# Queries and keys split into high and low part behind the transposition instead of ahead of it

## Chip, cores, metric

One core of a Trainium2 chip. The metric is the device time of one execution in microseconds, the median of the runs of a kernel; lower is better. Five engines work side by side, each on its own queue in order: TensorE (PE, its weight loads shown as PEld), VectorE (DVE), ScalarE (ACT), GpSimd (POOL), SyncE (SP, which issues nearly all DMAs here).

## The reference

Two pre-norm residual layers on x (256 tokens, 2048 channels, fp32). Layer A is sliding-window attention (window 128), layer B is native sparse attention: a compressed, a selected and a windowed branch, mixed by sigmoid gates. Both have 32 query heads of 64 dims in 4 key/value groups, a rotary embedding on the first 16 dims of queries and keys, and a SiLU gate ahead of the output projection:

```
proj = h @ w_in                                   # h = rmsnorm(x)
q = apply_rope(q, cos, sin);  k = apply_rope(k, cos, sin)
s = einsum('bqghd,bkgd->bghqk', q, k) * hd**-0.5  # then mask, softmax (A: with sinks)
o = einsum('bghqk,bkgd->bqghd', p, v)
x = x + (o * silu(z)) @ w_out
```

With 256 tokens all four blocks of 64 keys are selected, so the selected branch of B is plain causal attention.

## The kernel before

**Number format.** The projections and the scores run on PE in fp32r (a reduced fp32 that PE takes at full rate). To keep fp32 accuracy a tensor is split into a high part (an ACT copy that rounds to fp32r) and a low part (a DVE subtraction of the high part), and the products hi*hi, lo*hi, hi*lo are summed in PSUM. Weights are split this way too: `w_hi` by ACT and `w_lo` by DVE for each 512 KB block that arrives (`split`, L549).

**Loops.** The program is a list of steps, each a block of weights: for layer A keys and values, then for each of 4 groups the 512 query columns and the 512 gate columns (z), then the output projection; layer B likewise, with a small MLP that compresses keys and values and a gate projection in between. The products of a step with the activations make the `acc` matmuls. Attention runs in the background of these steps in units (g, t), g a group of 8 heads, t a tile of 128 tokens, so 8 units in each layer. A unit's front (`a_front` L812, `b_front` L1195) transposes its queries, multiplies them with the keys (tiles `s`) and does the softmax; its back transposes the probabilities (`pT`, fp32, with the fp32 identity, which lies in the tile `cst`), multiplies with the values (`pv`) and, in `finalize` (L706), applies the gate and splits the result into `aT_hi` and `aT_lo` for the output projection. In layer B the compressed branch adds the transposition `pcT` and the product `pv<-pcT,vbd`.

**Queries.** `post_q` (L627) runs when the projection of a group's queries for one token tile stands in PSUM: ACT copies it out with its scale (`q32`), POOL applies the rotation (`rope`, L613), ACT writes the high part and DVE the low part, both into one tile `qs` that holds high and low of each head side by side (128 columns a head). `q_transposed` (L639) then transposes each head's 128 columns, so that the high part lies on partitions 0 to 63 and the low part on 64 to 127 of `qT`: 8 fp32r transpositions with `identr` into two PSUM banks, and one ACT copy of each bank. A product with the keys, whose tile holds the same key part on both halves of the partitions, then sums high and low of the query at once.

**Keys.** `post_kv` (L666) does the same for 4 key heads: `key_stack` (L650) writes high (ACT) and low (DVE), each twice side by side, and `keys_to` (L658) transposes 4 + 4 blocks in fp32r into two banks with one ACT copy each. It runs for two token tiles in layer A, and for two in each of two key sets in layer B: 6 times.

**Buffers.** The ring `qs` has 2 tiles (4 KB a partition), the ring `q32` 2 (2 KB; also used by `side`, `th`, `low`, `junk`), the ring `qT` 2, the projection's PSUM banks `acc` 3, and the PSUM banks for all transpositions (`t_bank`, L357) 2.

**Order.** All instructions are recorded first. `Plan.order` (L247) then sets the order on each engine by simulating the queues with prices from `_price` (L164; a DVE instruction with 512 elements is priced at 612 ns there, a transposition in fp32 at about twice one in fp32r). Of the instructions of an engine that are ready by its clock, the one recorded first is taken; the weight splits go ahead of all, and `acc` matmuls fill what is left. PE work is treated as ready 0.8 us later than its inputs. So another price or another dependency moves rows far from the lines that were edited. The names of tiles in the trace are those of the program; since every instruction is recorded through one helper, all have the line L217.

Of the kernel before, what the change touches and what calls it, by code (L numbers as in the profile page):

```python
# [12 lines left out]
F32 = mybir.dt.float32  # L13
F32R = mybir.dt.float32r
# [6 lines left out]
P = 128  # L21
# [4 lines left out]
NG = 4  # L26
HPG = 8
HD = 64
NB = 512
# [310 lines left out]
def trunk(ctx: ExitStack, tc: tile.TileContext, x, positions, norm_w, final_norm_w,  # L340
# [4 lines left out]
    PE, ACT, DVE, POOL, SP = (Engine(plan, n, e) for n, e in (  # L345
        ("PE", nc.tensor), ("ACT", nc.scalar), ("DVE", nc.vector), ("POOL", nc.gpsimd), ("SP", nc.sync)))
    sb = Ring(plan, ctx.enter_context(tc.tile_pool(name="sb", bufs=1)))
# [6 lines left out]
    def s_bank(name):  # L354
        return pp.tile([P, NB], F32, tag="s", name=name, bufs=2)

    def t_bank(name, dt=F32):  # L357
        return pp.tile([P, 4, P], dt, tag="t", name=name, bufs=2)
# [4 lines left out]
    def copy(out, in_, scale=1.0):  # L363
        ACT.activation(out, in_, AF.Copy, scale=scale)
# [7 lines left out]
    ps = s_bank("idle")  # L372
# [8 lines left out]
    ident = cst[:, 0:P]  # L381
# [12 lines left out]
    identr = sb.tile([P, P], F32R, name="identr")  # L394
# [12 lines left out]
    for i, shift in enumerate((0.0, 0.25)):  # L407
# [3 lines left out]
        src = ang  # L411
        for c in TWO_PI:
            DVE.scalar_tensor_tensor(red[:, i], rnd[:, i], -c, src, op0=OP.mult, op1=OP.add)
            src = red[:, i]
# [37 lines left out]
    tb = t_bank("nwT")  # L452
# [4 lines left out]
    urgent, queue = deque(), deque()  # L457
# [40 lines left out]
    rq = [sb.tile([P, NT], F32, name=f"rq{i}") for i in range(2)]  # L498
# [114 lines left out]
    def rope(v, t, nh):  # L613

        tmp = sb.tile([P, 2, HPG, 16], F32, tag="rope", name="rope")
        a, b = tmp[:, 0, 0:nh, :], tmp[:, 1, 0:nh, :]

        def bc(tab, lo, n):
            return tab[:, t].rearrange("p a b -> p (a b)")[:, None, lo:lo + n].to_broadcast([P, nh, n])
        POOL.tensor_tensor(out=a, in0=v[:, :, 0:16], in1=bc(cs, 0, 16), op=OP.mult)  # L620
        POOL.tensor_tensor(out=b[:, :, 0:8], in0=v[:, :, 8:16], in1=bc(sn, 0, 8), op=OP.mult)
        POOL.tensor_tensor(out=b[:, :, 8:16], in0=v[:, :, 0:8], in1=bc(sn, 8, 8), op=OP.mult)
        POOL.tensor_tensor(out=v[:, :, 0:16], in0=a, in1=b, op=OP.add)

    qs = {}

    def post_q(layer, g):  # L627
        def post(t, ps):
            q32 = sb.tile([P, HPG, HD], F32, tag="q32", name="q32", bufs=2)
            copy(q32.rearrange("p h d -> p (h d)"), ps, scale=rq[layer][:, t:t + 1])  # L630
            rope(q32, t, HPG)
            s = sb.tile([P, HPG, 2, HD], F32R, tag="qs", name="qs", bufs=2)
            copy(s[:, :, 0, :], q32)
            DVE.tensor_sub(s[:, :, 1, :], q32, s[:, :, 0, :])
            qs[layer, g, t] = s
            flags.add(("q", layer, g, t))
        return post

    def q_transposed(layer, g, t):  # L639
        s = qs.pop((layer, g, t))  # L640
        qT = sb.tile([P, HPG, P], F32R, tag="qT", name="qT", bufs=2)
        for h in range(2):
            tb = t_bank("qT", F32R)
            for i in range(4):
                PE.transpose(tb[:, i, :], s[:, 4 * h + i].rearrange("p a d -> p (a d)"), identr)
            copy(qT[:, 4 * h:4 * h + 4, :], tb.bitcast(F32))
            yield 230.0
        return qT

    def key_stack(k32, n, name):  # L650

        s = sb.tile([P, 2, NG, 2, HD], F32R, tag="qs", name=name, bufs=2)
        src = k32[0:n, :, None, :].to_broadcast([n, NG, 2, HD])
        copy(s[0:n, 0], src)
        DVE.tensor_sub(s[0:n, 1], src, s[0:n, 0])
        return s

    def keys_to(kT, s, off):  # L658
        for hl in range(2):
            tb = t_bank("kT", F32R)  # L660
            for g in range(NG):
                PE.transpose(tb[:, g, :], s[:, hl, g].rearrange("p a d -> p (a d)"), identr)
            copy(kT[:, :, hl, off:off + P], tb.bitcast(F32))
            yield 230.0

    def post_kv(layer, kT, offs, vt):  # L666
        def post(t, ps):
            k32 = sb.tile([P, HPG, HD], F32, tag="q32", name="k32", bufs=2)[:, 0:NG]
            copy(k32.rearrange("p h d -> p (h d)"), ps[:, 0:256], scale=rms[layer][:, t:t + 1])
            DVE.tensor_scalar(vt()[:, t, :], ps[:, 256:512], rms[layer][:, t:t + 1], None, op0=OP.mult)  # L670
            rope(k32, t, NG)
            s = key_stack(k32, P, "kstack")
            urgent.append(keys_to(kT(), s, offs[t]))
        return post


# [135 lines left out]
    def a_front(g, t, kT, box):  # L812
        while ("q", 0, g, t) not in flags:
            yield None
        qT = yield from q_transposed(0, g, t)
        sms = []
        for par in range(2):
            sm = [sm_tile()]
            nm = sb.tile([P, 4], F32, tag="nm", name="nm", bufs=4)
            den = sb.tile([P, 4], F32, tag="den", name="den", bufs=4)  # L820
            yield from a_scores(g, t, kT, qT, par, sm, nm, den)
            sms.append(sm)
        box.append(sms)
# [371 lines left out]
    def b_front(g, t, box):  # L1195
        while ("q", 1, g, t) not in flags or "kcmp" not in flags or "gate" not in flags:
            yield None
        qT = yield from q_transposed(1, g, t)
        sms = []
        sc = sb.tile([P, HPG, 16], F32, tag="sc", name="sc", bufs=2)  # L1200
        for par in range(2):
            sm = [sm_tile() for _ in range(2)]
            nm = sb.tile([P, 2, 4], F32, tag="nmb", name="nmb", bufs=4)
            den = sb.tile([P, 2, 4], F32, tag="denb", name="denb", bufs=4)
            yield from b_scores(g, t, qT, par, sm, nm, den, sc)
            sms.append(sm)
        pc = cmp_softmax(g, t, sc)
        yield 0.0
        box.append((sms, pc))
# [73 lines left out]
    n = len(steps)  # L1283
# [72 lines left out]
```

## Time and profile before

| | |
|---|---|
| median of 3 runs | 799.94 us (799.88 to 800.97) |
| the profiled execution | 801.18 us, its span 799.5 us |
| PE busy | 783.0 us (98%), 4092 matmuls |
| DVE busy | 553.8 us (69%) |
| ACT busy | 479.1 us (60%) |
| POOL busy | 125.5 us (16%) |
| granted PE clock | 0.998 on average |
| DMA | 128.77 MB, mean 161 GB/s |

The page has the busy time of each engine, the chain of work that ended last (followed back from the last instruction through whatever released each step), and groups of instructions by operation and tile. PE's matmuls overlap in the records: a row's own duration is longer than the distance to the next row's start. What PE work costs is therefore read from the starts of rows that follow each other, or from the chain, whose pieces add up to the span.

### The profile page before, as it was taken

How to read it: one execution, taken by the hardware profiler on the slowest of the kernel's cores; microseconds unless marked ns; L12 is line 12 of the kernel's file. 1: busy time of each engine (PE TensorE's matmuls, PEld its weight loads, DVE VectorE, ACT ScalarE, POOL GpSimd, SP SyncE). 2: the span in 40 equal slices, each digit the busy share in tenths (PEclk: the TensorE clock that was granted, in tenths of full speed). 3: DMA queues.
4: the chain of work that ended last, by engine and by line, in shares of the span. 5: the costliest groups of instructions: out<-in, count | busy, mean ns of one | idle time of the engine just before them, and what ended most of it. 6: DMA issues, size and time to landing. Idle time of an engine off the chain costs nothing.

```text
span 799.5 us, 11784 instructions
## 1 busy us (share of the span) xinstructions
PE 783.0 (98%) x4092; PEld 631.8 (79%) x4092; DVE 553.8 (69%) x1148; ACT 479.1 (60%) x963; POOL 125.5 (16%) x169
## 2 busy tenths in 40 slices
PE   7999999999999999999999999999999999999995
PEld 4888878788788788888878887778868768777884
DVE  5657958858779655556756478858959868885572
ACT  6658657557476445554756486667658748654452
POOL 2102311213023000020101021111211021120110
PEclk9999999999999999999999999999999999999999
DMA  8655454654653555566667653544444444364652
GB/s 271 186 181 162 131 185 129 183 159 117 180 178 132 177 185 185 182 192 172 197 204 218 184 159 106 159 109 130 132 131 134 109 127 133 109 208 131 189 181 105
DMA packets 85995, 128.77 MB, mean 161 GB/s; under 512 B 6178, under 2 KB 43265, under 8 KB 85808
## 3 DMA queue, kind: packets, MB, share of 16 engines
q1 hardware_dynamic: 85536, 126.72, 52.4%
q0 software_dynamic: 400, 1.30, 0.6%
q8 instruction: 32, 0.52, 0.3%
q14 instruction: 27, 0.22, 0.1%
HBM read 125.91 MB, written 2.10 MB: 160 GB/s over the span
## 4 chain that ended last, share of the span: by engine, by line
PE 92%; DVE 3%; issue 2%; ACT 1%; DMA 1%; POOL 1%; SPq 0%; ACTq 0%; POOLq 0%; DVEq 0%
PE acc L217 75%; PE pv L217 5%; PE s L217 4%; PE pT L217 4%; PE qT L217 1%; DVE w_lo L217 1%; PE xT L217 1%; DMA raw<-in_a_w_in 1%; DVE sm L217 1%; ACT w_hi L217 1%; PE gates L217 1%; PE pcT L217 0%; PE kT L217 0%; PE mlp L217 0%; POOL rope L217 0%
## 5 line engine op out<-in xcount | busy, mean ns | idle before, releaser
L217 DVE TENSOR_TENSOR w_lo<-raw,w_hi 128x1024 fp32r<-128x1024 f32 (+1 forms) x231 | 294.0, 1275 | 154.8 <-ACT w_hi L217 151.7
L217 ACT ACTIVATE w_hi<-raw 128x1024 fp32r<-128x1024 f32 (+1 forms) x231 | 242.0, 1050 | 186.0 <-PE acc L217 149.3
L217 PE MATMUL acc<-w_hi,hT 128*128 128x512 f32 x768 | 247.6, 398 | 2.3 <-ACT w_hi L217 1.7
L217 PE MATMUL acc<-hT,w_hi 128*128 128x512 f32 x512 | 186.4, 399 | 0.0
L217 PEld LDWEIGHTS acc<-w_hi,hT 128*128 128x128 f32 x768 | 142.9, 189 | 37.9 <-issue 4.9
L217 PE MATMUL acc<-w_lo,hT 128*128 128x512 f32 x384 | 152.1, 396 | 0.0
L217 PE MATMUL acc<-hT,w_lo 128*128 128x256 f32 x512 | 143.7, 283 | 0.0
L217 PEld LDWEIGHTS acc<-hT,w_hi 128*128 128x128 f32 x512 | 96.2, 188 | 21.3 <-issue 3.2
L217 PEld LDWEIGHTS acc<-hT,w_lo 128*128 128x128 f32 x512 | 96.6, 189 | 0.7
L217 PE MATMUL acc<-w_hi,aT_hi 128*128 128x512 f32 x236 | 92.9, 394 | 0.8 <-ACT aT_hi L217 0.8
L217 PE MATMUL acc<-w_hi,aT_lo 128*128 128x512 f32 x236 | 92.6, 392 | 0.2 <-DVE aT_lo L217 0.2
L217 PE MATMUL acc<-w_lo,aT_hi 128*128 128x512 f32 x236 | 92.1, 391 | 0.0
L217 PEld LDWEIGHTS acc<-w_lo,hT 128*128 128x128 f32 x384 | 72.7, 189 | 18.5 <-issue 4.9
L217 ACT ACTIVATE sm<-sm,nmb 128x128 f32<-128x128 f32 (+1 forms) x128 | 56.9, 445 | 15.7 <-DVE nmb L217 15.1
L217 DVE CUSTOM_DVE_ANT_0 sm<-s,mask 128x128 f32<-128x128 f32 (+1 forms) x128 | 44.1, 349 | 20.6 <-PE s L217 20.4
L217 PEld LDWEIGHTS acc<-w_hi,aT_hi 128*128 128x128 f32 x236 | 44.3, 188 | 13.4 <-issue 2.4
L217 POOL TENSOR_TENSOR sm<-sm,denb 128x512 f32<-128x512 f32 (+1 forms) x16 | 29.3, 1832 | 151.2 <-DVE mx L217 60.8
L217 PEld LDWEIGHTS acc<-w_lo,aT_hi 128*128 128x128 f32 x236 | 44.3, 188 | 9.7 <-issue 0.8
L217 PEld LDWEIGHTS acc<-w_hi,aT_lo 128*128 128x128 f32 x236 | 44.3, 188 | 9.2 <-DVE aT_lo L217 0.5
L217 PE MATMUL s<-kTB,qT 128*128 128x272 f32 x192 | 39.2, 295 | 0.0
L217 PE MATMUL pT<-cst,sm 128*128 128x128 f32 x256 | 37.9, 275 | 0.5 <-DVE sm L217 0.2
L217 PEld LDWEIGHTS s<-kTB,qT 128*128 128x128 f32 x192 | 31.8, 188 | 7.4 <-issue 3.2
(187 smaller groups left out, 885.3 us busy)
## 6 DMA issues: line engine op xcount, KB each, us to landing
raw<-in_b_w_in SPq DMA_DIRECT2D x88, 512.0 KB, 3.7
raw<-in_a_w_in SPq DMA_DIRECT2D x72, 512.0 KB, 3.6
raw<-in_a_w_out SPq DMA_DIRECT2D x32, 512.0 KB, 3.6
raw<-in_b_w_out SPq DMA_DIRECT2D x32, 512.0 KB, 4.2
x<-in_x SPq DMA_DIRECT2D x8, 256.0 KB, 7.0
raw<-in_b_cmp_k_w SPq DMA_DIRECT2D x4, 512.0 KB, 3.8
raw<-in_b_cmp_v_w SPq DMA_DIRECT2D x4, 512.0 KB, 3.8
out<-x SPq DMA_DIRECT2D x4, 512.0 KB, 3.1
```

Source lines behind the costliest of these rows:

```text
L217: return getattr(eng.real, method)(*[real(a) for a in args], **{k: real(a) for k, a in kw.items()})
```

## The change

The rotated fp32 queries are kept whole. Two heads lie side by side in 128 columns, so 4 fp32 transpositions bring the 8 heads of a unit into one PSUM bank (an even head on partitions 0 to 63, an odd one on 64 to 127). The split comes behind: two ACT copies of 64 partitions x 512 elements write the high parts in place, and two DVE subtractions of the same size write the low parts onto the other half of the partitions. Keys are written out twice in fp32 by one ACT copy, transposed by 4 fp32 transpositions into one bank, and split by one ACT copy and one DVE subtraction from PSUM. The fp32 tiles of queries and keys now come from the ring `qs` and stay there until they are transposed. One call of `q_transposed` or `keys_to` now ends with one piece of 440 ns for the background's budget; there were two of 230.

```diff
     def post_q(layer, g):
         def post(t, ps):
-            q32 = sb.tile([P, HPG, HD], F32, tag="q32", name="q32", bufs=2)
-            copy(q32.rearrange("p h d -> p (h d)"), ps, scale=rq[layer][:, t:t + 1])
-            rope(q32, t, HPG)
-            s = sb.tile([P, HPG, 2, HD], F32R, tag="qs", name="qs", bufs=2)
-            copy(s[:, :, 0, :], q32)
-            DVE.tensor_sub(s[:, :, 1, :], q32, s[:, :, 0, :])
-            qs[layer, g, t] = s
+            q = sb.tile([P, 2, NB], F32, tag="qs", name="q", bufs=2)[:, 0]
+            copy(q, ps, scale=rq[layer][:, t:t + 1])
+            rope(q.rearrange("p (h d) -> p h d", d=HD), t, HPG)
+            qs[layer, g, t] = q
             flags.add(("q", layer, g, t))
         return post
 
     def q_transposed(layer, g, t):
-        s = qs.pop((layer, g, t))
-        qT = sb.tile([P, HPG, P], F32R, tag="qT", name="qT", bufs=2)
-        for h in range(2):
-            tb = t_bank("qT", F32R)
-            for i in range(4):
-                PE.transpose(tb[:, i, :], s[:, 4 * h + i].rearrange("p a d -> p (a d)"), identr)
-            copy(qT[:, 4 * h:4 * h + 4, :], tb.bitcast(F32))
-            yield 230.0
-        return qT
-
-    def key_stack(k32, n, name):
-
-        s = sb.tile([P, 2, NG, 2, HD], F32R, tag="qs", name=name, bufs=2)
-        src = k32[0:n, :, None, :].to_broadcast([n, NG, 2, HD])
-        copy(s[0:n, 0], src)
-        DVE.tensor_sub(s[0:n, 1], src, s[0:n, 0])
-        return s
-
-    def keys_to(kT, s, off):
-        for hl in range(2):
-            tb = t_bank("kT", F32R)
-            for g in range(NG):
-                PE.transpose(tb[:, g, :], s[:, hl, g].rearrange("p a d -> p (a d)"), identr)
-            copy(kT[:, :, hl, off:off + P], tb.bitcast(F32))
-            yield 230.0
+
+
+        q = qs.pop((layer, g, t))
+        qT = sb.tile([P, 4, 2, P], F32R, tag="qT", name="qT", bufs=2)
+        tb = t_bank("qT")
+        for i in range(4):
+            PE.transpose(tb[:, i, :], q[:, i * P:(i + 1) * P], ident)
+        for par in range(2):
+            copy(qT[ROWS[par], :, par, :], tb[ROWS[par]])
+        for par in range(2):
+            DVE.tensor_sub(qT[ROWS[1 - par], :, par, :], tb[ROWS[par]], qT[ROWS[par], :, par, :])
+        yield 440.0
+        return qT.rearrange("p i a s -> p (i a) s")
+
+    ROWS = [slice(par * HD, (par + 1) * HD) for par in range(2)]
+
+    def keys_to(kT, twice, off):
+
+        tb = t_bank("kT")
+        for g in range(NG):
+            PE.transpose(tb[:, g, :], twice[:, g].rearrange("p a d -> p (a d)"), ident)
+        hi = kT[:, :, 0, off:off + P]
+        copy(hi, tb)
+        DVE.tensor_sub(kT[:, :, 1, off:off + P], tb, hi)
+        yield 440.0
 
     def post_kv(layer, kT, offs, vt):
         def post(t, ps):
-            k32 = sb.tile([P, HPG, HD], F32, tag="q32", name="k32", bufs=2)[:, 0:NG]
+            both = sb.tile([P, 2 * HPG, HD], F32, tag="qs", name="k32", bufs=2)
+            k32 = both[:, 0:NG]
             copy(k32.rearrange("p h d -> p (h d)"), ps[:, 0:256], scale=rms[layer][:, t:t + 1])
             DVE.tensor_scalar(vt()[:, t, :], ps[:, 256:512], rms[layer][:, t:t + 1], None, op0=OP.mult)
             rope(k32, t, NG)
-            s = key_stack(k32, P, "kstack")
-            urgent.append(keys_to(kT(), s, offs[t]))
+            twice = both[:, HPG:2 * HPG].rearrange("p (g a) d -> p g a d", a=2)
+            copy(twice, k32[:, :, None, :].to_broadcast([P, NG, 2, HD]))
+            urgent.append(keys_to(kT(), twice, offs[t]))
         return post
```

Since the order is planned, the rows move. Three places.

**PE, the first queries of layer A.** `acc` are the gate columns' products (512 columns with `w_hi`, 256 with `w_lo`), `s` the scores of the first unit. Before:

```order
L217 MATMUL acc_652<-hT,w_lo 128x256
L217 MATMUL qT<-identr,qs 128x128 x8
L217 MATMUL acc_670<-hT,w_hi 128x512
L217 MATMUL acc_670<-hT,w_lo 128x256
L217 MATMUL acc_670<-hT,w_hi 128x512
L217 MATMUL acc_670<-hT,w_lo 128x256
L217 MATMUL acc_670<-hT,w_hi 128x512
L217 MATMUL acc_670<-hT,w_lo 128x256
L217 MATMUL acc_670<-hT,w_hi 128x512
L217 MATMUL acc_670<-hT,w_lo 128x256
L217 MATMUL acc_652<-hT,w_hi 128x512
L217 MATMUL s<-kTA,qT 128x256 x2
```

And now:

```order
L217 MATMUL qT<-cst,q 128x128 x4
L217 MATMUL acc_656<-hT,w_lo 128x256
L217 MATMUL acc_656<-hT,w_hi 128x512
L217 MATMUL acc_656<-hT,w_lo 128x256
L217 MATMUL acc_638<-hT,w_hi 128x512
L217 MATMUL acc_638<-hT,w_lo 128x256
L217 MATMUL acc_638<-hT,w_hi 128x512
L217 MATMUL acc_638<-hT,w_lo 128x256
L217 MATMUL acc_638<-hT,w_hi 128x512
L217 MATMUL acc_638<-hT,w_lo 128x256
L217 MATMUL acc_638<-hT,w_hi 128x512
L217 MATMUL qT<-cst,q 128x128 x4
```

The eight fp32r transpositions of the first unit, and two later groups of four for the second, have become four in fp32 for each of the two token tiles. The first group stands earlier in the gate columns than it did, the second unit is transposed ahead of the first unit's scores, and those come 21 rows after the last row shown: 11520 columns of `acc` lie between a first group and its `s` (3584 before). In all 16 + 6 groups of four fp32 transpositions stand where there were 128 + 48 fp32r ones.

**DVE, the second group of layer B.** `qT` is the new subtraction, `w_lo` the low part of weights, `u<-u,pv` the previous unit's finalize, the ISA rows the new unit's masked scores. Now:

```order
L217 TENSOR_TENSOR w_lo<-raw,w_hi 128x1024 x2
L217 TENSOR_TENSOR qT<-qT 64x4x128 x2
L217 TENSOR_TENSOR w_lo<-raw,w_hi 128x1024
L217 TENSOR_TENSOR u<-u,pv 128x4x128
L217 ISA sm,nmb<-s,mask 128x128
```

Ahead of these scores stood, at the same place of the groups before, two subtractions `qs<-q,qs` with a `w_lo` in between; the second unit's pair of new subtractions follows 39 and 52 rows later, among the first unit's scores.

**PE, the end of layer B's attention.** `pv<-pcT,vbd` is the last attention product; the output projection's `acc` follows. Before:

```order
L217 MATMUL pv<-pcT,vbd 128x512
L217 MATMUL acc_7248<-w_hi,aT_hi 128x512
L217 MATMUL acc_7248<-w_hi,aT_lo 128x512
L217 MATMUL acc_7248<-w_lo,aT_hi 128x512
L217 MATMUL acc_6971<-w_hi,aT_hi 128x512
```

And now:

```order
L217 MATMUL acc_6832<-w_lo,aT_hi 128x512
L217 MATMUL acc_7101<-w_hi,aT_hi 128x512
L217 MATMUL acc_7101<-w_hi,aT_lo 128x512
L217 MATMUL acc_7101<-w_lo,aT_hi 128x512
L217 MATMUL acc_7101<-w_hi,aT_hi 128x512
L217 MATMUL acc_7101<-w_hi,aT_lo 128x512
L217 MATMUL acc_7101<-w_lo,aT_hi 128x512
L217 MATMUL acc_6863<-w_hi,aT_hi 128x512
```

`acc_6971` before and `acc_6863` now are the first that need the last unit's `aT_hi` (second token tile, first output columns). Three products stood between the last `pv<-pcT,vbd` and it; now there are 14 (8 of `acc_6832`, of which the last is shown, and 6 of `acc_7101`).

## Rows read from the trace of the kernel before

**Rows 1.** The page: busy time of each engine, and the chain that ended last by engine.

```profile
PE 783.0 (98%) x4092; PEld 631.8 (79%) x4092; DVE 553.8 (69%) x1148; ACT 479.1 (60%) x963; POOL 125.5 (16%) x169
...
PE 92%; DVE 3%; issue 2%; ACT 1%; DMA 1%; POOL 1%; SPq 0%; ACTq 0%; POOLq 0%; DVEq 0%
```

**Rows 2.** Busy time in stretches: from, to, length, then PE, PEld, DVE, ACT, POOL with instructions, granted PE clock, DMA share, GB/s. A group of layer A, a group of layer B, then three parts of the latter.

```profile
115.00:169.00 54.00, 53.96 (x294) 44.18 (x293) 40.95 (x84) 33.71 (x70) 11.66 (x14) 1.00 0.52 157
571.00:637.00 66.00, 65.92 (x371) 51.86 (x370) 52.04 (x145) 44.54 (x109) 11.52 (x14) 1.00 0.46 127
598.00:620.00 22.00, 22.00 (x142) 19.01 (x141) 20.99 (x79) 18.30 (x55) 2.93 (x3) 1.00 0.49 143
620.00:626.00 6.00, 6.00 (x35) 4.46 (x34) 2.59 (x16) 4.72 (x14) 0.00 (x0) 1.00 0.31 87
626.00:649.00 23.00, 22.85 (x113) 17.75 (x112) 22.22 (x46) 13.43 (x30) 5.14 (x3) 1.00 0.52 139
```

**Rows 3.** The chain that ended last in order of time: start us, length us, what. The first group of layer A, then one place of layer B.

```profile
66.59 0.64 PE qT L217 x8
69.77 0.29 PE qT L217 x4
81.95 0.44 PE pT L217 x4
...
498.07 0.66 PE pT L217 x4
```

**Rows 4.** The same chain at the first keys.

```profile
41.77 0.30 PE kT L217 x4
```

**Rows 5.** PE in order of time: start us, duration us, instruction. A group of fp32r transpositions and what follows it.

```profile
69.61 0.46 PE L217 MATMUL qT<-identr,qs 128*128 128x128 f32 x4
69.90 0.35 PE L217 MATMUL acc<-hT,w_lo 128*128 128x256 f32 x1
70.09 0.40 PE L217 MATMUL acc<-hT,w_hi 128*128 128x512 f32 x1
70.33 0.28 PE L217 MATMUL acc<-hT,w_lo 128*128 128x256 f32 x1
70.44 0.39 PE L217 MATMUL acc<-hT,w_hi 128*128 128x512 f32 x1
```

**Rows 6.** The same for a group of fp32 transpositions.

```profile
81.79 0.60 PE L217 MATMUL pT<-cst,sm 128*128 128x128 f32 x4
82.14 0.47 PE L217 MATMUL acc<-hT,w_hi 128*128 128x512 f32 x1
82.46 0.28 PE L217 MATMUL acc<-hT,w_lo 128*128 128x256 f32 x1
```

**Rows 7.** Groups of instructions by form, PE, ACT and DVE: operation, tiles, shape, count, busy us, mean ns, idle before.

```profile
L217 PE MATMUL qT<-identr,qs 128*128 128x128 f32 x128 | 14.7, 245 | 0.0
L217 PE MATMUL kT<-identr,kstack 128*128 128x128 f32 x48 | 5.7, 241 | 1.2 <-ACT kstack L217 1.2
...
L217 ACT ACTIVATE qT<-qT 128x512 fp32r<-128x512 f32 x32 | 18.3, 587 | 1.6 <-PE qT L217 1.6
L217 ACT ACTIVATE qs<-q 128x512 fp32r<-128x512 f32 x16 | 10.0, 626 | 2.5 <-POOL q L217 2.5
L217 ACT ACTIVATE kTB<-kT 128x512 fp32r<-128x512 f32 x8 | 4.5, 594 | 0.0
L217 ACT ACTIVATE room<-kcT 64x256 f32<-64x256 f32 x4 | 1.5, 378 | 1.8 <-PE kcT L217 1.6
...
L217 DVE TENSOR_TENSOR w_lo<-raw,w_hi 128x1024 fp32r<-128x1024 f32 x225 | 289.6, 1289 | 153.3 <-ACT w_hi L217 150.1 <-PE acc L217 2.2
L217 DVE TENSOR_TENSOR qs<-q,qs 128x512 fp32r<-128x512 f32 x16 | 12.2, 765 | 0.0
L217 DVE TENSOR_TENSOR u<-u,pv 128x512 f32<-128x512 f32 x16 | 11.0, 685 | 4.7 <-PE pv L217 4.4
L217 DVE TENSOR_TENSOR kstack<-k,kstack 128x512 fp32r<-128x512 f32 x6 | 4.5, 749 | 1.8 <-ACT kstack L217 1.8
L217 DVE COPY room<-kcT 64x256 f32<-64x256 f32 x4 | 1.6, 427 | 0.1
```

**Rows 8.** What PE waited for in the whole span: us in total, times, longest.

```profile
PE kT L217 <- ACT kstack L217: 1.2, 2, 0.8
PE mlp L217 <- DVE w_lo L217: 1.0, 2, 0.5
PE acc L217 <- ACT aT_hi L217: 0.8, 1, 0.8
```

**Rows 9.** PE in order of time at the end of layer B's attention.

```profile
723.59 0.39 PE L217 MATMUL acc<-w_lo,aT_hi 128*128 128x512 f32 x1
724.73 0.50 PE L217 MATMUL acc<-w_hi,aT_hi 128*128 128x512 f32 x1 [0.75 <-ACT aT_hi L217]
725.46 0.50 PE L217 MATMUL acc<-w_hi,aT_lo 128*128 128x512 f32 x1 [0.22 <-DVE aT_lo L217]
```

**Rows 10.** DVE in order of time: copies of the upper 64 partitions behind a full-width subtraction, and in the busy stretch of a group of layer B a weight's low part while POOL scales probabilities.

```profile
374.01 1.23 DVE L217 TENSOR_TENSOR w_lo<-raw,w_hi 128x1024 fp32r<-128x1024 f32 x1 [1.40 <-ACT w_hi L217]
375.27 0.77 DVE L217 COPY room<-kcT 64x256 f32<-64x256 f32 x2
...
642.46 2.92 DVE L217 TENSOR_TENSOR w_lo<-raw,w_hi 128x1024 fp32r<-128x1024 f32 x1
```

## The prediction

> **What bounds the kernel now.** I read the busy times and the chain first, then stretches of the program, then the price of each piece of PE's work in place, and last the waits. PE is busy in 98% of the span and holds 92% of the chain; DVE comes second with 69% and 3% [rows 1]. A group of layer A and one of layer B show the same locally: PE 53.96 of 54.00 us and 65.92 of 66.00, DVE 41 and 52, ACT 34 and 45, the granted clock 1.00 [rows 2]. So time on PE counts in full, and time on ACT or DVE counts only where PE comes to wait. In the whole span PE waits little at places the change touches: 1.2 us in two pieces at `kT`, 0.8 at the last `aT_hi` [rows 8]. Inside B's group DVE is nearly full from 598 to 620 (20.99 of 22) and from 626 (22.22 of 23), with 3.4 us of idle time between (2.59 busy of 6.00) [rows 2]. There a later DVE could reach PE.
>
> **Term 1: transpositions, on PE's path.** Before, 128 fp32r transpositions of queries and 48 of keys run [rows 7]. Four of them hold 0.29 to 0.30 us of the chain, eight 0.64 [rows 3, 4], so 0.075 each. Each group also makes the next product dearer: 256 columns take 0.19 behind one (69.90 to 70.09) and 0.11 otherwise (70.33 to 70.44) [rows 5], so about 0.07 a group. The order has 27 groups of queries and 12 of keys: 128 x 0.075 + 27 x 0.07 = 11.5, and 48 x 0.075 + 12 x 0.07 = 4.4, together 15.9 us.
>
> Afterwards 16 + 6 groups of four fp32 transpositions stand there. The nearest row is `pT`: fp32, the same 128x128 tiles, the same identity. Four hold 0.44 in the chain [rows 3]; in time order 0.35 to the next start, and the 512 columns behind them take 0.32 in place of 0.24 [rows 5, 6], so 0.43: the two agree. 22 x 0.44 = 9.7. **Gain 15.9 - 9.7 = 6.2 us.** Bounds: without the 0.07 a group in the old price 13.2 - 9.7 = 3.5; with the bare 0.36 a new group 15.9 - 7.9 = 8.0. I take 6.2 since chain and starts both contain the follow-up cost.
>
> **Term 2: the end of layer B.** Behind the last product that doesn't need the last unit's `aT`, PE starts at 724.73 in place of 723.59 + 0.24, and once more at 725.46 in place of 724.97 [rows 9]: 0.90 + 0.49 = 1.4 us idle. The order now puts 14 products, 14 x 0.24 = 3.4 us, where 3 (0.7) stood. That is 2.7 more cover than the wait is long. **Gain 1.4**, bounds 0 (if the last `aT` comes as much later as the products were moved up) to 1.4.
>
> **Term 3: the keys of layer B.** PE waits 0.8 and, of 1.2 in all, 0.4 again for `kstack` [rows 8]. The chain to it was product, ACT copy, POOL rotation, ACT high part, DVE low part; PE named only the ACT part. Now the twofold ACT copy comes last, and the low part moves behind the transposition (ACT 0.594, DVE 0.75 before [rows 7]). PE's wait is for the same ACT step, but one group fewer (0.37) lies ahead of the second token tile, so each pair can wait 0.3 to 0.4 longer. **Loss 0.4**, bounds 0 and 0.8 (both waits longer by 0.4).
>
> **Term 4: DVE later in B's groups.** A query unit gives up `qs` at 0.765 and gets two subtractions of 64x512 from PSUM. `u<-u,pv`, which has PSUM and SBUF inputs and 512 columns too, takes 0.685 [rows 7]; half the partitions I price as all of them, as 64x256 takes ACT 378 ns, well over half the 587 of 512 columns on 128 [rows 7]. So +0.6 a unit, +1.2 a group, 9.7 in sixteen units; in keys a 0.75 subtraction becomes one of the same size. Most of the 1.2 is covered by the 3.4 us of idle time in mid-group [rows 2]; without that cover it shows. PE's `pT` groups of the first back end in B already hold 0.66 where four cost 0.44 [rows 3], 0.22 of waiting at four places. I let them grow by 0.15 each: **loss 0.6**, bounds 0 and 4 x 1.2 = 4.8. I stay near the low end because mid-group idle time is three times the addition.
>
> **At nothing.** ACT loses 0.626 a query unit and 0.594 a key call [rows 7] (two copies of half the partitions for two of all), some 13.6 us; it is 60% busy and PE rarely waits for it. POOL does the same rotations, SP's queue keeps its order. The ring `qs` has two tiles still, now free only after the transposition, as before. The longer way to the scores is covered by the gate columns' products; that cover is rival A's question.
>
> **Sum.** -6.2 - 1.4 + 0.4 + 0.6 = -6.6 us. The profiled execution took 801.18 us, of which the span is 799.5; that is 1.24 above the median of the runs. 801.18 - 6.6 = 794.6 profiled, so 799.94 - 6.6 = **793.3 us** as the median.
>
> **A rule against the change.** DVE's overlap of neighbouring instructions is seen in the trace: two copies of the upper half behind each other are over in 0.77 us [rows 10], where one is recorded at 0.427 on average [rows 7]; the first of them starts at 375.27, only after the end (375.24) of the full-width subtraction ahead of it. The Trainium skill, "VectorE: DVE Perf Modes", section "Two Vector instructions with no wait between them", has a rule for this: an instruction whose inputs or output start in another quadrant of partitions than the last ones' is held until all earlier Vector instructions are finished. By that rule each of the two shifted subtractions and the full-width instruction after them is held. By the rule that adds an estimated three times 0.085 (2 x 0.427 - 0.77), so 0.26 a unit and 0.5 a group of DVE's time, and the sum would be unchanged while mid-group idle time holds, and belongs to rival B otherwise.
>
> **Rivals.**
>
> *A, slower (chance 0.06): the scores wait for the low parts.* The split now stands between transposition and scores: two ACT copies (2 x 0.59 [rows 7]), two subtractions (2 x 0.685), and what stands ahead on those queues: a `w_lo` of 1.29 on average, up to 2.92 while POOL scales [rows 7, 10]. For it: that is 3.8 to 5.5 us in a row before the last low part is written. Against it: the order puts 11520 columns, 15 x (0.24 + 0.11) = 5.2 us [rows 5], between a first group and its scores in A. Price: where 1.0 us shows in each of 16 units, 16 - 6.6 = +9.4, so 809.3 us. It makes the kernel slower from (6.6 + 1.6)/16 = 0.5 us a unit on.
>
> *B, same (0.11): DVE hands its extra work on.* If the busy stretches of B's groups pass on the 1.2 us a group, and half as much again of one subtraction where POOL's scaling doubles DVE's times (2.92 against 1.29 [rows 7, 10]), instead of 0.15, four groups give 4 x 1.5 = 6.0 in place of 0.6: about 798.7 us. For it: DVE holds 95% of 598 to 620 and 97% of 626 to 649 [rows 2]. Against it: the idle 3.4 between, and the second unit's pair stands among the first's scores, after the busiest place.
>
> *C, slower (0.02): an fp32 transposition costs as four fp32r ones.* 88 x 4 x 0.075 + 22 x 0.07 = 28.0 in place of 15.9: +12.1 in place of -6.2, so 811.6 us. Against it stands `pT`, fp32 as well, at 0.11 each [rows 3]. The Trainium skill, "FP8 and Floating Point Precision", section "TensorE Precision Notes", says that true fp32 takes four passes through the array; by this the time would be rival C's, and the `pT` rows of this trace do not agree for transpositions.
>
> *D, faster still (0.08): ACT's relief and the moved rows also remove waits elsewhere.* `mlp` waits 1.0 us for `w_lo` [rows 8], the four `pT` places 0.9 [rows 3], and with terms 3 and 4 at zero (1.0) that is 2.9 more: 799.94 - 9.5 = 790.4 us.
>
> That the change doesn't do what it says is excluded by the order, which has 22 groups of four fp32 transpositions.
>
> **How the numbers follow.** The forecast has what is left, 0.73. Its own unknowns, term 1 by +2.7 or -1.8 and term 4 up to +4.2, rarely fall together. The range goes from 790.5, above D's end, to 798.0, where term 1 is at its low end and term 4 and 3 somewhat up (793.3 + 2.7 + 2.0), near B; outside lie A, C, half of B or a little more, and half of D: 0.19. The measurement can tell 0.2% here, 1.6 us: faster below 798.3, which is the forecast, D, and none of B counted: 0.81; the same B's 0.11; slower A and C, 0.08.
>
> **What would show it.** Right: PE has 88 fewer transpositions of queries and keys, groups of `qT<-cst,q` and `kT<-cst` hold about 0.44 in the chain, no wait of PE at `acc<-aT_hi`, `s` waits for no `qT`, DVE's busy time grows by about 9, ACT's falls by about 13. Wrong: waits of PE at `s` for DVE's `qT` (A), longer waits at `pT` for `sm`, `pt` or `denb` with DVE full across 620 to 626 (B), or groups of four at over 1 us (C). A median above 798.3 would make the forecast wrong.

## The result, and the profile after

The changed kernel takes 793.11 us in the median (792.27 to 793.6, 4 runs) beside 800.37 for the kernel before in the same comparison: ratio 0.9905, interval 0.989 to 0.992, so 6.4 to 8.8 us faster. A second comparison gave 792.48 beside 800.79, 0.9898 (0.9881 to 0.9914). The forecast was 793.3, in a range of 790.5 to 798.0. It had counted 6.6 us off 799.94, the median known then; measured side by side the change is worth 7.3 and 8.3 us in the two comparisons.

The profiled execution took 793.6 us, its span 791.5 (before 801.18 and 799.5). First the page: busy times, and the chain that ended last by engine, to be held against [rows 1].

```profile
PE 775.1 (98%) x4004; PEld 625.8 (79%) x4004; DVE 562.3 (71%) x1164; ACT 466.0 (59%) x941; POOL 122.9 (16%) x169
...
PE 88%; DVE 5%; issue 3%; ACT 1%; DMA 1%; POOL 1%; SPq 0%; ACTq 0%; POOLq 0%; DVEq 0%
```

PE has 88 matmuls fewer and is busy for 7.9 us less, ACT for 13.1 us less, DVE for 8.5 us more. PE is still the bound, but more of the chain now runs over DVE. Next, what PE waited for in the whole span (us in total, times, longest), against [rows 8].

```profile
PE xT L217 <- DMA x<-in_x: 2.4, 2, 2.0
...
PE mlp L217 <- DVE w_lo L217: 1.0, 2, 0.5
PE pT L217 <- DVE sm L217: 0.8, 3, 0.3
PE kT L217 <- ACT k L217: 0.8, 2, 0.4
...
PE pT L217 <- DVE pt L217: 0.2, 1, 0.2
```

The waits at the last `aT` are gone, those at `kT` are 0.8 in place of 1.2, those at `pT` have grown, and `s` waits for nothing. The line at `mlp` is as it was. (`xT` and most lines left out lie at the start. The traces after and before reach the first product of a projection at 9.95 and 10.07 us, and the hundredth `acc` product 29.9 and 29.7 us later, so the start favours neither. It does vary from one execution to the next: a second trace of the changed kernel gets there in 28.8 us and keeps this 1.1 us to the end.)

The groups by form that answer to [rows 7]:

```profile
L217 PE MATMUL qT<-cst,q 128*128 128x128 f32 x64 | 9.6, 273 | 0.0
L217 PE MATMUL kT<-cst,k 128*128 128x128 f32 x24 | 3.7, 277 | 0.8 <-ACT k L217 0.8
L217 DVE TENSOR_TENSOR qT<-qT 64x512 fp32r<-64x512 f32 x32 | 22.0, 688 | 5.0 <-ACT qT L217 4.1
L217 ACT ACTIVATE qT<-qT 64x512 fp32r<-64x512 f32 x32 | 18.9, 592 | 9.2 <-PE qT L217 8.7
```

Half the partitions cost as much as all: a 64x512 copy takes ACT 592 ns (128x512: 587 [rows 7]), a 64x512 subtraction takes DVE 688 (128x512: 685 [rows 7]). A group of the new transpositions in PE's order of time, against [rows 5]:

```profile
64.02 0.60 PE L217 MATMUL qT<-cst,q 128*128 128x128 f32 x4
64.37 0.36 PE L217 MATMUL acc<-hT,w_lo 128*128 128x256 f32 x1
64.57 0.40 PE L217 MATMUL acc<-hT,w_hi 128*128 128x512 f32 x1
```

Four fp32 transpositions take 0.35 to the next start, and the 256 columns behind them 0.20 in place of 0.11: 0.44 all in, as taken from `pT`. By single starts, three of the four distances are 0.109 and the last is 0.029, so what looked like a price of the product behind is about the rest of the fourth transposition. The end of layer B's attention, against [rows 9]:

```profile
712.63 0.39 PE L217 MATMUL pv<-pcT,vbd 128*128 128x512 f32 x1
712.86 0.39 PE L217 MATMUL acc<-w_hi,aT_lo 128*128 128x512 f32 x1
```

Products follow each other every 0.23 us from here on, and PE does not wait again up to the end of the layer.

To add up all of PE's time, each instruction can be given the distance from its start to the next start, with the waits taken out (its start distance). Over both spans this makes 10.30 us of query transpositions before and 5.73 after, 3.70 and 2.24 of key transpositions: -6.0 of the span's -8.0 us.

### The profile page after: what moved, and what is told of

It reads as the page before. It is cut to its first block, busy times and chain, and to the rows that moved or that the text cites. A ratio compares the mean times of both kernels' runs of the same rounds, so it can differ in the third digit from the quotient of the medians.

```text
span 791.5 us, 11613 instructions
## 1 busy us (share of the span) xinstructions
PE 775.1 (98%) x4004; PEld 625.8 (79%) x4004; DVE 562.3 (71%) x1164; ACT 466.0 (59%) x941; POOL 122.9 (16%) x169
## 4 chain that ended last, share of the span: by engine, by line
PE 88%; DVE 5%; issue 3%; ACT 1%; DMA 1%; POOL 1%; SPq 0%; ACTq 0%; POOLq 0%; DVEq 0%
PE acc L217 72%; PE pv L217 5%; PE s L217 4%; PE pT L217 4%; DVE sm L217 2%; DVE w_lo L217 1%; PE qT L217 1%; PE xT L217 1%; DMA raw<-in_a_w_in 1%; DVE u L217 1%; ACT w_hi L217 1%; PE gates L217 1%; PE pcT L217 0%; POOL rope L217 0%; PE mlp L217 0%
## 5 line engine op out<-in xcount | busy, mean ns | idle before, releaser
L217 PEld LDWEIGHTS acc<-w_lo,aT_hi 128*128 128x128 f32 x236 | 44.3, 188 | 11.3 <-issue 2.4
L217 PEld LDWEIGHTS acc<-w_hi,aT_hi 128*128 128x128 f32 x236 | 44.3, 188 | 9.7 <-ACT w_hi L217 0.8
L217 PEld LDWEIGHTS acc<-w_hi,aT_lo 128*128 128x128 f32 x236 | 44.3, 188 | 8.9
L217 PEld LDWEIGHTS pT<-cst,sm 128*128 128x128 f32 x256 | 30.0, 140 | 13.8 <-issue 5.4
```

The source lines that it names most:

```text
L217: return getattr(eng.real, method)(*[real(a) for a in args], **{k: real(a) for k, a in kw.items()})
```

## The experiments

**Queries alone and keys alone.** Two kernels, each with one half of the diff.

> Only the queries are changed; the keys are split ahead of their transposition as before. Its order has the 14 products of cover at the end of layer B. Theory (the terms of the prediction, queries' share): 128 fp32r transpositions become 64 in fp32 (10.3 us to 5.7 by the starts of the two traces, -4.6), 11 groups fewer with 0.07 of follow-up (-0.8), no wait at the last aT (-1.4), waits at pT (+0.6): about -6.2, so 794.2 with before at 800.4. Rival (the keys carry what the two traces show between the start of layer B and its last keys, 3.4 us, and the queries only the rest): about -4, 796.4.

Measured 793.99 us (before 800.29; ratio 0.9922, 0.9909 to 0.9934): -6.3, as expected.

> Only the keys are changed; queries as before. Its order has the 3 products of cover at the end, as before. Theory: 48 fp32r transpositions become 24 in fp32 (3.7 us to 2.2, -1.5), 6 groups fewer with 0.07 of follow-up (-0.4), and waits at kT as the changed kernel shows them, 0.76 in place of 1.22 (-0.4): about -2.3, 798.1; PE still waits about 1.0 us for the last aT. Rival (the prediction's term 3): the waits at kT grow by 0.4, about -1.5, 798.9. Rival (keys carry the 3.4 us between the traces): 797.0.

Measured 798.33 us (ratio 0.9975, 0.9965 to 0.9984): -2.0, among the three expectations. Its interval takes in the first two of them, and the waits decide for the theory: those at `kT` did not grow. Waits of PE in the two kernels, queries alone first:

```profile
PE kT L217 <- ACT kstack L217: 1.2, 2, 0.8
...
PE pT L217 <- DVE sm L217: 0.6, 2, 0.3
```

```profile
PE kT L217 <- ACT k L217: 0.8, 2, 0.4
PE acc L217 <- ACT aT_hi L217: 0.8, 1, 0.8
...
PE pT L217 <- DVE sm L217: 0.2, 1, 0.2
```

The waits part cleanly: the new keys shorten those at `kT`, the new queries lengthen those at `pT` and, by the order they lead to, remove those at the last `aT`. -6.3 and -2.0 make -8.3, against -7.3 and -8.3 in the two comparisons of the whole. The last rival (that the keys carry the 3.4 us by which the two traces differ up to the last keys of layer B) rested on a misreading: that stretch ends at an instruction that moved. Ahead of it lie 28 products of the gate projection before and 14 after.

**Transpositions of queries twice.**

```
-        for i in range(4):
+        for i in (0, 1, 2, 3) * 2:
             PE.transpose(tb[:, i, :], q[:, i * P:(i + 1) * P], ident)
```

> The changed kernel with each unit's four fp32 transpositions of queries issued twice into the same bank, 64 more in 16 groups. Theory (PE is the bound, a group of four costs what it takes on PE): 16 x 0.36 to 0.44 = +5.8 to +7.0, so 798.9 to 800.1. Rival (transpositions of queries lie beside waits, so that the saving came from elsewhere): under +2, below 795.1. By fp32 at four fp32r passes: 64 x 0.30 = +19, 812.

Measured 800.93 us, +7.8 over the changed kernel: 0.8 above the expected end. In the trace the query transpositions take 12.66 us by start distances in place of 5.73, so +6.9, which is 16 x 0.43, or 4 x 0.108 a group. The rest are new waits, of the scores and of `pT`:

```profile
PE s L217 <- DVE nmb L217: 0.8, 3, 0.3
...
PE pT L217 <- DVE pt L217: 0.7, 3, 0.2
```

So PE's price of a group shows in full in the time. Rival C (four fp32r prices each, +19) falls.

**The low parts twice.**

```
-        for par in range(2):
+        for par in (0, 1) * 2:
             DVE.tensor_sub(qT[ROWS[1 - par], :, par, :], tb[ROWS[par]], qT[ROWS[par], :, par, :])
```

> The changed kernel with each of the 32 shifted subtractions done twice: 22 us more on DVE, and the way from transposition to scores longer by 2 x 0.69 = 1.4 us a unit. Its planned order again has only 4 products of cover at the end, so +1.0 to +1.4 there. Theory (the low parts are covered, DVE has room): that and at most 1.5 us of waits at pT, 794.1 to 796. Rival A (scores wait for the low parts): 16 x 1.4 = +22, 815. Rival B (DVE full in the groups of layer B): 8 x 1.4 = +11, 804.

Measured 814.15 us (ratio 1.0171, 1.0157 to 1.0184), +21: the theory that DVE has room failed outright. The waits of PE:

```profile
PE pT L217 <- POOL sm L217: 6.6, 8, 1.2
PE acc L217 <- DVE denb L217: 2.4, 2, 1.2
...
PE s L217 <- DVE nmb L217: 1.7, 2, 0.9
PE s L217 <- DVE qT L217: 1.3, 2, 0.7
```

Only 1.3 us of these waits are scores that wait for `qT`; the rest is the softmax and what follows it, which come late over DVE and POOL. In one place PE also ran at its lower clock behind them (last section). Eight of the waits (6.6 us) lie in layer A, where DVE was busy for only 41 of 54 us before [rows 2]. Is it the way to the scores, DVE's time, or the order, which is planned anew with the added instructions? Half the dose, then the same dose off the way, then that with the old order:

```
-        for par in range(2):
+        for par in (0, 1, 1):
             DVE.tensor_sub(qT[ROWS[1 - par], :, par, :], tb[ROWS[par]], qT[ROWS[par], :, par, :])
```

> The changed kernel with one of each unit's two shifted subtractions done twice: half of the dose that cost 21 us, the way to the scores 0.69 longer a unit, DVE 11 us more. Its order has lost the 14 products of cover at the end (+1.0 to +1.4). Theory now (the cover between transposition and scores has an edge that the full dose crossed): under +4, 794.1 to 797. Rival A in the prediction's form (what the way takes, shows, without an edge): 16 x 0.65 = +10.5, so 803.6.

Measured 799.45 us, +7.0 beside 792.48 for the changed kernel on the same chip; between the two expectations. Neither had its cause right: it is not a price for each unit, and the cover that was thought lost at the end of layer B costs nothing here (PE waits for no `aT` in this trace). Most of it hangs on one place, a wait of 2.4 us at `pT` in the last group of layer B:

```profile
PE pT L217 <- DVE sm L217: 2.8, 2, 2.4
```

Behind it PE runs at the lower of its two clocks for a while (last section), which costs about as much again; the two make some 5.3 us of the 7.

> The changed kernel with two more subtractions of 64x512 a unit on DVE whose result nobody reads, recorded behind the two real ones: DVE gets some 22 to 24 us, as in the double dose, but the scores do not wait for them. If the way to the scores was what cost 21 us: +1 to +4, 794 to 797. If DVE's queue was it (rival B): +11 to +21, 804 to 814.

```
...
+        for par in range(2):
+            hi = qT[ROWS[par], :, par, :]
+            DVE.tensor_sub(spare[ROWS[par]].rearrange("p (i s) -> p i s", s=P), hi, hi)
```

(`spare` is the unused half of the `qs` tile.) Measured 816.96 us (814.72 to 818.33 in four runs), +24.5. No score waits for `qT` in its trace, so a loss of this size comes without a longer way to the scores.

> As the run with DVE work off the way (two more subtractions of 64x512 a unit that nobody reads), but priced at 1 ns where the order is planned, so that every row of PE stands as in the changed kernel. If DVE's time in its queue is what cost 24 us there: about as much again, 810 to 818 where the changed kernel is 792.5. If the changed order was it: 793.5 to 797.

```
+        if self.free_of_charge:
+            op.cost = 1
...
```

(The flag is set around the two added subtractions alone. PE, ACT and POOL then have exactly the changed kernel's order, and DVE has it with 32 rows added.)

Measured 802.32 us (ratio 1.0028, 1.0017 to 1.0038): +9.8 over the changed kernel. This lies between my two expectations and splits the 24.5: about 10 us are DVE's added time in the unchanged order, about 15 the order that the planner made of it, with the clock that fell behind its longer waits. The waits that remain in the unchanged order (the helper's line is L218 here):

```profile
PE s L218 <- DVE nm L218: 3.7, 4, 0.9
...
PE acc L218 <- DVE u L218: 1.4, 2, 0.8
PE s L218 <- DVE nmb L218: 1.3, 2, 0.9
```

The first line is one wait of 0.9 a group in layer A, though DVE idles there for a fifth of the group on average (44.3 us busy of 54.6). It comes at the end of a stretch that is full. The stretch up to the first of them, at 80.57 us, and the one ahead of it (columns as in [rows 2]):

```profile
50.00:65.00 15.00, 15.00 (x75) 12.59 (x74) 6.71 (x6) 7.68 (x9) 3.39 (x8) 1.00 0.61 186
65.00:80.60 15.60, 14.67 (x92) 12.71 (x90) 15.08 (x42) 11.44 (x31) 1.04 (x1) 1.00 0.52 156
```

DVE is busy for 6.7 of 15 us, and in the next 15.6 for 15.1, while PE idles for 0.9. The idle time ahead does not help the scores behind it.

**Less DVE work.**

```
...
+            if par:
+                copy(lo, tb[ROWS[par]], scale=0.0)
+            else:
+                DVE.tensor_sub(lo, tb[ROWS[par]], qT[ROWS[par], :, par, :])
```

> The changed kernel, but the low part of the odd heads is written as zeros by an ACT copy of the same size: one shifted subtraction a unit less, DVE 11 us less, ACT 9.5 us more; it leaves out the correction of half of the heads. With the single and double dose this makes a curve of DVE's load: -11, 0, +11 (7.0 us), +22 (21.7 us). Theory (an edge: the load that the change adds lies just below where DVE's queue begins to show): -1.0 (the waits at pT) to +1.4 (another order at the end of layer B), so 791.5 to 793.9. Rival (no edge, DVE's load shows at 0.6 us per us throughout): -6 to -7, about 786.

Measured 795.02 us (ratio 0.9933, 0.992 to 0.9945; the changed kernel 0.9898): 2 to 3 us slower with 16 subtractions, 11 us, less on DVE. Both expectations missed. Its planned order has new waits, which ACT's added copies and the moved rows share:

```profile
PE pT L217 <- DVE sm L217: 1.2, 3, 0.7
...
PE pT L217 <- ACT sm L217: 0.6, 1, 0.6
...
PE s L217 <- DVE sc L217: 0.4, 1, 0.4
```

So there is no clean curve of DVE's load here: every such edit is an edit of the order too.

**Keys two heads at a time.** The queries' way, used on the keys: 2 transpositions a call, no twofold copy ahead.

```
+        for i in range(2):
+            PE.transpose(tb[:, i, :], k32[:, 2 * i:2 * i + 2, :].rearrange("p a d -> p (a d)"), ident)
+        kk = kT.rearrange("p (i a) h k -> p i a h k", a=2)
+        for par in range(2):
+            for r in (par, 1 - par):
+                copy(kk[ROWS[r], :, par, 0, off:off + P], tb[ROWS[par], 0:2])
...
+                DVE.tensor_sub(kk[ROWS[r], :, par, 1, off:off + P], tb[ROWS[par], 0:2],
+                               kk[ROWS[par], :, par, 0, off:off + P])
```

> The changed kernel again, beside the next three on one chip: 792.5 to 793.8, before at 800.3.

> The changed kernel with keys also transposed two heads at a time: 2 fp32 transpositions a call in place of 4, no twofold ACT copy ahead of them, and behind them four ACT copies and four DVE subtractions of 64x256. The end of layer B keeps its 14 products of cover. Theory: 12 transpositions less at 0.09 to 0.11 (-1.1 to -1.3) and the waits of 0.43 and 0.33 at kT gone, as the twofold copy (0.59) no longer stands ahead (-0.8): -2.0, so 791.1 where the changed kernel is 793.1. Rival: the eight smaller instructions (8 x 0.38 to 0.43 in place of 0.59 + 0.68 a call) hold up weights' low parts on DVE or the scores: 0 to +2.

Measured 790.33 us (ratio 0.9871, 0.9856 to 0.9885) beside 792.48 for the changed kernel: -2.15, as expected in size, and the fastest version here. The waits moved less than thought:

```profile
PE kT L217 <- POOL k L217: 0.6, 2, 0.4
PE mlp L217 <- DVE w_lo L217: 0.5, 2, 0.3
```

At `kT` PE now waits for the rotation itself; the wait at `mlp` gave back the other half us.

**A truer price.** The same kernel, with the shifted subtractions priced at 720 ns in the planning.

> Keys two heads at a time as in the run at 790.3, and the shifted subtractions priced at 720 ns in the planning of the order (612 before), which is their distance in the trace. The order of PE changes in many places, and at the end of layer B it again has few products of cover. Theory: the waits at pT (1.1) go, the wait at the last aT (1.0 to 1.4) comes back: 790.0 to 791.0. Rival (a truer price makes a better order throughout): below 789.5.

Measured 794.8 us (ratio 0.993, 0.9916 to 0.9943), 4.5 us slower, outside both expectations. The wait at `pT` for `sm` did go, and the one at the end came back:

```profile
PE acc L218 <- DVE u L218: 0.7, 3, 0.2
...
PE acc L218 <- ACT aT_hi L218: 0.5, 1, 0.5
...
PE acc L218 <- DVE aT_lo L218: 0.2, 1, 0.2
```

These and the restart of PE behind them explain some 2 us. At the end of layer A its trace already is 3.1 us behind: 1.3 of these come in the first 11 us of products, where two executions of the changed kernel differ by 1.1, and 1.9 later, where PE does not wait in either trace. There the start distances of `acc<-w_hi,hT` (+1.4) and `pv` (+0.6) grew with the new order; why was not traced.

## Why the prediction was right, point by point

**Term 1** (-6.2): right in mechanism and a little small, and shown three ways. Directly -6.0, to which the prediction's follow-up costs (39 x 0.07 before, 22 x 0.08 after) add about -1.0, so some -7.0; queries alone -6.3 with terms 2 and 4; and doubling the new groups cost 0.43 each where 0.44 was taken. The old transpositions were a little dearer than taken (0.080 for a query's, 10.30/128, in place of 0.075). An fp32 one costs 0.109 with its follow-up, not four times an fp32r one. The Trainium skill, "FP8 and Floating Point Precision", section "TensorE Precision Notes", has four passes for true fp32; these rows do not agree with that for transpositions.

**Term 2** (-1.4): right. The waits of 0.75 and 0.22 [rows 9] are gone where the order has the 14 products of cover: gone with the queries alone, there with the keys alone, whose order has 3.

**Term 3** (+0.4): wrong sign; -0.4 came. The step that failed is "PE's wait is for the same ACT step", with the way to it held fixed. It became shorter: the rotation on POOL ahead of it took 3.15 us before and takes 2.75 now. (The "one group fewer" ahead of it counted for less than 0.37: at the first of the two places the order put one more product there, and PE's work between the two calls is 3.03 us in place of 3.10; at the second it is 2.95 in place of 3.21.) Before, on POOL and DVE:

```profile
397.28 0.89 POOL L217 TENSOR_TENSOR rope<-k,cs 128x64 f32<-128x64 f32 x1 [2.64 <-ACT k L217]
398.13 0.91 POOL L217 TENSOR_TENSOR rope<-k,sn 128x32 f32<-128x32 f32 x2
399.12 1.31 POOL L217 TENSOR_TENSOR k<-rope 128x64 f32<-128x64 f32 x1
...
397.91 0.81 DVE L217 TENSOR_TENSOR kstack<-k,kstack 128x512 fp32r<-128x512 f32 x1
...
399.03 1.21 DVE L217 TENSOR_TENSOR w_lo<-raw,w_hi 128x1024 fp32r<-128x1024 f32 x1
```

After:

```profile
393.93 0.89 POOL L217 TENSOR_TENSOR rope<-k,cs 128x64 f32<-128x64 f32 x1 [2.64 <-ACT k L217]
394.79 1.49 POOL L217 TENSOR_TENSOR rope<-k,sn 128x32 f32<-128x32 f32 x2
396.36 0.32 POOL L217 TENSOR_TENSOR k<-rope 128x64 f32<-128x64 f32 x1
...
394.96 1.21 DVE L217 TENSOR_TENSOR w_lo<-raw,w_hi 128x1024 fp32r<-128x1024 f32 x1
396.09 0.68 DVE L217 TENSOR_TENSOR kTB<-kT,kTB 128x512 fp32r<-128x512 f32 x1
```

The last step of the rotation takes 0.32 in place of 1.31. Before, it ran beside a `w_lo` and ended 0.19 behind it (400.43 and 400.24); that `w_lo` came so late because `kstack` stood ahead of it on DVE. Now `kstack` is gone from that stretch, the `w_lo` ends at 396.17, beside the middle steps, and the last step runs free beside a subtraction that reads PSUM and SBUF. The run with the keys alone has the same times (0.32 for the last step), the one with the queries alone the old ones (1.30). That POOL slows down beside DVE subtractions that read two tiles of SBUF is what the rows suggest; no run here tried it by itself.

**Term 4** (+0.6): the size is right (waits at `pT` from 0.2 to 1.0), its reason only half. The 0.22 of waiting "at four places" was a misreading of the chain: the whole trace before has one wait at `pT`, of 0.17 at 498.07, and the same piece of 0.66 stands at 564.78 and 580.23 without any. The 3.4 us of idle time in mid-group were named as the cover. With the order held fixed, the next 22 us of DVE work cost 10 us, 0.45 of each, although average idle time is far larger. The change's 9.7 us were nearly free, but the margin beyond them was not what I took it for: rival B, given 0.11, was nearer than its chance says.

**The rule on held instructions** (the Trainium skill, "VectorE: DVE Perf Modes", section "Two Vector instructions with no wait between them") agrees with the trace. On DVE, in layer A and then in B:

```profile
67.48 2.12 DVE L217 TENSOR_TENSOR qT<-qT 64x512 fp32r<-64x512 f32 x3
69.63 1.22 DVE L217 TENSOR_TENSOR w_lo<-raw,w_hi 128x1024 fp32r<-128x1024 f32 x1
...
564.86 0.68 DVE L217 TENSOR_TENSOR u<-u,pv 128x512 f32<-128x512 f32 x1
565.46 1.22 DVE L217 TENSOR_TENSOR w_lo<-raw,w_hi 128x1024 fp32r<-128x1024 f32 x1
```

Three shifted subtractions of 0.688 take 2.12 and the next starts after their end; a full-width one of 0.68 lets the next start after 0.60. So each starts 0.72 behind the one before, in place of 0.60: 0.1 a hold, as estimated, 0.3 a unit.

**Rival A** did not come: no `s` waits for `qT` in the changed kernel, 1.3 us do with the low parts twice. **Rival D** neither: `mlp` waits 1.0 as before, and `pT` waits longer.

**The sum.** By these measures the terms make -7.0 - 1.4 - 0.4 + 0.8 = -8.0, the difference of the two spans, where -6.6 was forecast. The median of 793.11 lies closer to 793.3 than that, by luck: this comparison gave 7.3, and its kernel before was 0.4 above the 799.94 that the forecast started from.

**What the prediction left out:** it priced the new order only at the end of layer B. The runs with another planned order (+15 of the 24.5 off the way, +3 to +4.5 with the truer price, +2 to +3 with less DVE work) show that the moved rows can weigh as much as the whole gain. That this change drew an order without such losses was not argued from any row: there luck had a part.

## What to carry to other kernels

Where PE is full, as here, its removed work can be priced by start distances of the nearest rows, and it shows in full. Idle time of a second engine counts only where it lies behind the work that is added and ahead of what waits: look at stretches of 15 us, not at the group's mean. Where a planner sets the order, a change of one price or one instruction is a change of the order; test a cost with the order held fixed as well, or it is put down to the wrong thing.

## What was not expected of the hardware

PE's granted clock, 1.00 from 20 us to the end of both layers in the traces before and after, falls to its lower level (0.50, which is 1.2 of 2.4 GHz) in some places where an added load makes PE wait. With one low part twice, PE idled for 0.38 and then 2.44 us ahead of 675.2; the stretch before, the one behind it and a later one (columns as in [rows 2]):

```profile
668.00:674.00 6.00, 4.24 (x26) 3.34 (x24) 5.84 (x25) 4.33 (x17) 1.04 (x1) 1.00 0.28 93
675.20:681.00 5.80, 5.80 (x23) 5.17 (x23) 4.54 (x18) 2.64 (x7) 1.16 (x2) 0.50 0.01 3
682.00:688.00 6.00, 6.00 (x37) 4.41 (x36) 4.21 (x10) 4.61 (x11) 0.00 (x0) 1.00 0.25 89
```

At 0.50 for 5.8 us, PE loses an estimated 2.9 us of work (5.8 x 0.50): about as much as the two waits together, 2.8. With both low parts twice, three shorter waits close together (0.19, 0.86 and 0.86 us, the last up to 552.12) were followed by it too:

```profile
553.00:556.30 3.30, 3.30 (x13) 2.73 (x12) 3.10 (x12) 2.20 (x5) 1.39 (x1) 0.50 0.03 7
```

The single waits of up to 0.9 us in the run with PE's order held were not. In the run off the way, the same two waits (0.6 and 1.9 us) come three times: behind 551.73 and 622.03 the clock fell (0.53 and 0.61 on average over the next 3 to 4 us), behind 692.54 it stayed at 1.00. So the length of the waits alone does not tell, and what does is open.
